# Modulation products moved between engines and stages, a new head for the first FFNs, and more PSUM banks in turn

## The chip, the cores and the metric

The kernel is one launch on one core of a Trainium2 chip. The metric is device time in microseconds, the median of several runs. The engines are TensorE (PE, matrix products; PEld is its loading of weights), VectorE (DVE), ScalarE (ACT), GpSimd (POOL) and SyncE (SP), whose queue issues the transfers. Each engine takes its instructions in order from its own queue and waits for others by semaphores. Matrix products write into PSUM, which the kernel splits into eight banks of 128x512 float32, and everything else lies in SBUF.

## The reference

A first block of two layers (a state space mixer beside latent attention, attention to a memory, a gated FFN), then a second block of two layers on the result (attention over neighbours or a window, a gated FFN), whose norms are modulated by a vector `c`, with a context stream `ctx` beside `x`. Everything is float32. Shapes: 512 tokens of 1024 for `x`, 256 for `ctx`, FFN width 2816, so `w_up` gives 2 x 22 tiles of 128 channels. The parts that the change touches:

```python
# first block, at the end of each layer
x = x + memory_attention(rmsnorm(x, g_q), rmsnorm(mem, g_kv), ...)
u = causal_dwconv(rmsnorm(x, norm_ffn[i]) @ w_up[i], conv_w, conv_b)   # 3 taps
gate, val = u[..., :D_FF], u[..., D_FF:]
x = x + (silu(gate) * val) @ w_down[i]
# second block, layer i: needs all six parts of mod, of x and (not in the last layer) of ctx
mod = silu(c) @ w_mod[i] + b_mod[i]            # 1024 -> 6 x 1024
mod_c = silu(c_ctx) @ w_mod[i] + b_mod[i]
sh1, sc1, gt1, sh2, sc2, gt2 = split(mod)
h = rmsnorm(x, g_attn[i]) * (1 + sc1) + sh1
x = x + gt1 * (attention(h, ...) @ w_out)
h = rmsnorm(x, g_ffn[i]) * (1 + sc2) + sh2
x = x + gt2 * conv_ffn(h, ...)                 # the same for ctx in layer 0
```

`mod` is a product of a matrix with one vector. The kernel computes it off TensorE: a tile of 128 rows and 512 columns of `w_mod` is multiplied by `silu(c)` element by element and summed along the row.

## The kernel before

Activations lie transposed, channels on partitions: `x` is eight tiles of 128 x 512 tokens. TensorE gets each float32 operand in two parts, a high half rounded to its format and a low half, the rest: for weights `wh` and `wl`, and likewise for activations (both named `A` in the traces, as most temporary tiles are). A product of one 128 x 128 weight block with one x tile is three matrix products: wh times high, wh times low, wl times high (`lin`, L298). A tile of 1024 inputs so takes 24 products. `wload` (L317) brings a weight tile into `wr` by an SP transfer, makes `wh` on ScalarE (L314) and `wl` on VectorE (L331); there are two `wr` and three each of `wh` and `wl`, so a tile's halves are made at most a few tiles ahead. `gsplit` (L437, L438) makes the halves of an x tile, scaled by the norm's gain.

In time order the program is: for each of two layers mixer, `mem_attn`, `ffn1`; then the context and neighbourhood attention of the second block, `attn_out`, `ffn2` for both streams, the window attention, `attn_out_halves`, `ffn2` for `x` alone.

`ffn1` (from L1155) runs `F1_PARTS`: 6, 6, 5 and 5 of the 22 gated pairs. A pair `j` is two up tiles (`up`): 24 products into a bank (`L`, `S`, `PT` in turn), on VectorE a product with the norm's factor `rs` out of the bank (L1178), the first tap of the convolution on ScalarE (L1181), two taps on VectorE (L1183), then silu (L1185), gate (L1186) and the split (L314, L317). The down tiles of a part are queued and run between the pairs of the next part; each ends with an addition into `x` on VectorE (L1199). The sum of squares for the norm comes from GpSimd and ScalarE; TensorE adds it over the channels by products with `ones`, VectorE takes the inverse root in ten small steps on 128 x 4 numbers (`rt`, L394, L369 to L379), and TensorE spreads that over the partitions (`O<-cm,rt`). At the start of `ffn1` the first up tile waits for the last x tile of `mem_attn`, and the norm's spread is placed in the midst of the second tile.

The modulation is a side job: `mod_steps` (L1250) is a generator, and `step(n, r)` takes from it at fixed places of other stages, with `after` holding the instruction back to the matrix product issued before it. Of eight products two are a `scalar_tensor_tensor` with a sum on VectorE (L1282), six a GpSimd product (L1284) with a copy and sum on ScalarE behind it (L1262). Layer 0 of the first block makes all of `mod[0]`, layer 1 all of `mod[1]`: one step for each of the eight `w_mo` tiles of `mem_attn`, then 2 or 5 a pair in `ffn1`. The tiles of `w_mod` are loaded four steps ahead, into the pool of 59 `A` tiles.

`ffn2` (L2000) in layer 0 has both streams: an up weight tile serves 24 products 256 wide (`ctx`) and 24 products 512 wide (`x`). Its parts are 8, 7 and 7 pairs, then 16 down outputs each. All go through two buffers of bank `L`. At the end of a part `lins` runs the first down outputs without the last activation tile, then that tile's products.

The order of each engine's instructions around these places is fixed by a scheduler at build time, from the order of the code and the holds.

Of the kernel before, what the change touches and what calls it, by code (L numbers as in the profile page):

```python
# [14 lines left out]
AF = mybir.ActivationFunctionType  # L15
# [21 lines left out]
PSTEP = (5,3,1)  # L37
MSTEP = (0,1,4,1,2)
MDN = (0,0,2)
MH = 48  # L40
MLAG = 3
FX = 1
# [19 lines left out]
PIN = 1  # L62
MPF = 4
MODV = (0,4)
WP = 0
# [21 lines left out]
F1_PARTS = ((0, 6), (6, 6), (12, 5), (17, 5))  # L87
F1_MOD = (2, 5, 5, 5)
F1_KEEP = 2
# [169 lines left out]
class Builder:  # L259
# [263 lines left out]
    def mixer(self, i, f, fn):  # L523
# [215 lines left out]
        for tb in range(4):  # L739
            row = []  # L740
            for hf in range(2):
                ps = self.p("S")
                for k in range(2):
                    ch, cl = ckh[k]
                    s = slice(tb * P, tb * P + P)
                    w = slice(k * 512, k * 512 + 512)
                    self.mm(ps, ch[:, s], wv[hf][0][:, w], k == 0, False)
                    self.mm(ps, ch[:, s], wv[hf][1][:, w], False, False)
                    self.mm(ps, cl[:, s], wv[hf][0][:, w], False, k == 1)
                vt = self.t("A", [P, S])  # L750
                nc.scalar.activation(vt, ps, AF.Copy)
                row.append(vt)
            V.append(row)
# [310 lines left out]
    def mem_attn(self, i, f, mh, K, fn):  # L1064
# [16 lines left out]

        self.steps = self.mod_steps(i, 0, 96)
        mv = self.mem_v(i, mh, V)
# [64 lines left out]


    def step(self, n, r):  # L1150
# [6 lines left out]
    def ffn1(self, i, f, fn):  # L1157
# [3 lines left out]
        self.wp = WP  # L1161
        self.bank = 0

        def bank():
            self.bank += 1
            return self.p(FTAGS[self.bank % len(FTAGS)])

        def up(j):
            ab = []
            for e in range(2):  # L1170
                ct = j + NFF * e
                ps = bank()
# [72 lines left out]

    def mod_steps(self, i, n0, n1):
        nc = self.nc
        cv = []
        for v in range(2):
            for e in range(2):  # L1250
# [4 lines left out]
            yield  # L1255
        part = self.mparts
        late = []

        def add(k):
            while len(late) > k:  # L1260
                o, t = late.pop(0)
                nc.scalar.activation(t, t, AF.Copy, accum_out=o)  # L1262

        ws = {}

        def load(n):
            if n < n1:
                ws[n] = self.t("A", [P, 512])
                nc.sync.dma_start(out=ws[n], in_=self.a["w_mod"][i, n // 2, n % 2])

        for n in range(n0, n0 + MPF):
            load(n)
        for n in range(n0, n1):
            load(n + MPF)
            m, e = divmod(n, 2)
            w = ws.pop(n)
            for v in range(2):
                t = self.t("A", [P, 512])
                self.modn += 1
                o = part[:, v, e, m:m + 1]  # L1280
                if self.modn % 8 in MODV:
                    nc.vector.scalar_tensor_tensor(out=t, in0=w, scalar=1.0, in1=cv[2 * v + e], op0=ALU.mult, op1=ALU.mult, accum_out=o)  # L1282
# [3 lines left out]
            add(MLAG)  # L1286
            yield
        add(0)
        if n1 == 96:
            for v in range(2):  # L1290
                mo = self.mod[i][:, :, v]
                nc.vector.tensor_add(out=mo, in0=part[:, v, 0], in1=part[:, v, 1])
                nc.vector.tensor_add(out=mo, in0=mo, in1=self.v(f"b_mod{i}"))
            for j, gn in ((0, "g_attn"), (1, "g_ffn")):
                for s in range(2):
                    nc.vector.scalar_tensor_tensor(out=self.G[i][j][:, :, s], in0=self.mod[i][:, 24 * j + 8:24 * j + 16, s], scalar=1.0,
                                                   in1=self.v(f"{gn}{i}"), op0=ALU.add, op1=ALU.mult)
            yield
# [640 lines left out]

    def out_it(self, i, m, ox, k0, k1):  # L1940
        n = k1 - k0
        w = self.wload(self.a[f"w_o2{i}"][m, :, k0 * P:k1 * P], n * P)
        ps = self.p("L")
        yield from self.lin_it(ps, w, ox[k0:k1])
        self.nc.vector.scalar_tensor_tensor(out=self.x[:, m], in0=ps, scalar=self.msl(i, 2, m, 0), in1=self.x[:, m], op0=ALU.mult, op1=ALU.add)
# [54 lines left out]
    def ffn2(self, i, rx, rc, acc, accc, steps=iter(()), late=None):  # L2000
# [3 lines left out]
        if rc is not None:  # L2004
            streams[1] = (rc, ML)
        w, ab = {}, {}

        def up(j, e, s, tag="L"):
# [3 lines left out]
            ps = self.p(tag)  # L2012
            self.lin(ps[:, :n], w[j, e], rhs)
# [21 lines left out]

        for pi, (j0, nj) in enumerate(FF_PARTS):
            act = {s: [] for s in streams}
            last = pi == len(FF_PARTS) - 1
            first = 0
            if pi == 0 and rc is not None and FX:  # L2040

                for j, e, s in ((0, 0, 1), (0, 1, 1), (1, 0, 1), (0, 0, 0), (0, 1, 0), (1, 1, 1), (1, 0, 0), (1, 1, 0)):
                    up(j, e, s, "S" if s else "L")
                    if e == 1:
# [31 lines left out]
            def down(m, s):  # L2076
# [3 lines left out]
                else:  # L2080
                    ps = self.p("L")
                    self.lin(ps[:, :n], weights(m), act[s])
# [10 lines left out]
            for z, (m, s) in enumerate(order[:DW]):  # L2093
                pss[m, s] = self.p(DT2[z % len(DT2)])
# [79 lines left out]
    def build(self):  # L2174
        self.setup()
        self.modn = 0
        self.mod_prep()
# [46 lines left out]
```

## Time and profile before

| | us |
|---|---|
| median of 3 runs | 3841.25 |
| lowest and highest | 3839.11, 3844.32 |
| profiled execution | 3832.78 |
| its span | 3831.0 |
| PE busy | 3675.2 (96%) |
| DVE busy | 2669.1 (70%) |
| ACT busy | 1842.9 (48%) |
| POOL busy | 1001.0 (26%) |

The profile is of one execution. Its span goes from the first to the last instruction; the profiled execution's time lies 1.8 us above it. A row of a stretch gives for each engine the busy time and, in brackets, the number of instructions; PEclk is the granted clock as a share of 2.4 GHz. In a timeline, brackets tell how long the engine stood idle before the instruction and what released it.

### The profile page before, as it was taken

The numbers are of one execution on the slowest core, as the hardware profiler recorded it, in microseconds if no ns is written. First come the engines' busy times: TensorE is split into PE (matmuls) and PEld (weight loads), VectorE is DVE, ScalarE is ACT, GpSimd is POOL, SyncE is SP. The second block draws the span as 40 slices with busy tenths as digits, with TensorE's granted clock in tenths as the row PEclk, the third lists the DMA queues.
The fourth block names the chain that finished last, engine by engine and source line by source line (L and its number), as shares of the span: only waits on it lengthen the run. The fifth ranks groups of instructions, "written<-read, shape, count | busy, mean of one in ns | idle before, by whom it ended". The sixth has DMA issues, their size and how long they took to land. (4 is left out here: it accounts for less than half of the span.)

```text
span 3831.0 us, 55553 instructions
## 1 busy us (share of the span) xinstructions
PE 3675.2 (96%) x21300; PEld 3062.5 (80%) x21300; DVE 2669.1 (70%) x4599; ACT 1842.9 (48%) x3532; POOL 1001.0 (26%) x688
## 2 busy tenths in 40 slices
PE   8999999999899999999999899899999999999999
PEld 6777788777778777887777899778888888888887
DVE  7768756889977687668998753777545547657555
ACT  5645634455555456344555454774222225554232
POOL 1223243467621121234666212321000012100000
PEclk9999999999999999999999999999999999999999
DMA  3222143344422211333444332322212212012232
GB/s 112 67 72 67 51 127 100 111 154 157 146 91 72 72 57 56 126 105 102 165 155 150 123 104 92 108 73 72 66 61 61 66 56 74 15 40 93 94 95 93
DMA packets 128714, 354.39 MB, mean 93 GB/s; under 512 B 14144, under 2 KB 26816, under 8 KB 128448
## 3 DMA queue, kind: packets, MB, share of 16 engines
q1 hardware_dynamic: 127440, 349.62, 28.6%
q8 instruction: 168, 2.75, 0.3%
q10 hardware_dynamic: 1008, 1.21, 0.1%
q14 instruction: 98, 0.80, 0.1%
HBM read 346.58 MB, written 4.19 MB: 92 GB/s over the span
## 5 line engine op out<-in xcount | busy, mean ns | idle before, releaser
L304 PE MATMUL L<-A,wh 128*128 128x512 f32 (+1 forms) x6408 | 1861.5, 375 | 19.5 <-ACT wh L314 8.8
L304 PEld LDWEIGHTS L<-A,wh 128*128 128x128 f32 x6408 | 1148.0, 189 | 241.7 <-ACT wh L314 13.1
L304 PE MATMUL L<-A,wl 128*128 128x512 f32 (+1 forms) x3204 | 1194.9, 373 | 20.4 <-DVE wl L331 19.8
L314 ACT ACTIVATE wh<-wr 128x1024 fp32r<-128x1024 f32 (+4 forms) x562 | 561.9, 1001 | 787.7 <-PE L L304 429.8
L331 DVE TENSOR_TENSOR wl<-wr,wh 128x1024 fp32r<-128x1024 f32 (+4 forms) x503 | 658.7, 1311 | 327.2 <-ACT wh L314 319.1
L304 PEld LDWEIGHTS L<-A,wl 128*128 128x128 f32 x3204 | 604.7, 189 | 137.5 <-DVE wl L331 26.3
L1284 POOL TENSOR_TENSOR A<-A,A 128x512 f32<-128x512 f32 x288 | 482.3, 1706 | 280.6 <-DMA A<-in_w_mod 169.2
L304 PE MATMUL S<-A,wh 128*128 128x512 f32 (+1 forms) x944 | 301.0, 400 | 25.6 <-ACT wh L314 14.7
L331 POOL TENSOR_TENSOR wl<-wr,wh 128x1024 fp32r<-128x1024 f32 (+1 forms) x59 | 139.4, 2363 | 547.4 <-ACT wh L314 473.4
L304 PE MATMUL L<-wh,A 128*128 128x256 f32 x1440 | 272.7, 285 | 2.3 <-ACT A L1309 2.0
L304 PE MATMUL PT<-A,wh 128*128 128x512 f32 (+1 forms) x904 | 262.1, 375 | 0.0
L304 PEld LDWEIGHTS S<-A,wh 128*128 128x128 f32 x944 | 180.9, 195 | 70.8 <-ACT wh L314 16.5
L1183 DVE SCALAR_TENSOR_TENSOR A<-A,vec,A 128x512 f32<-128x512 f32 x176 | 215.2, 1223 | 30.6 <-ACT A L1181 26.4
L304 PEld LDWEIGHTS L<-wh,A 128*128 128x128 f32 x1440 | 226.0, 189 | 8.1 <-issue 4.2
L304 PE MATMUL O<-A,A 128*64 128x128 f32 (+3 forms) x2528 | 228.1, 288 | 4.2 <-DVE A L648 3.6
L433 POOL TENSOR_TENSOR acc<-acc,A 128x512 f32<-128x512 f32 (+1 forms) x44 | 53.8, 1222 | 672.1 <-ACT A L427 670.2
L304 PE MATMUL L<-wl,A 128*128 128x256 f32 x720 | 204.6, 284 | 4.6 <-DVE wl L331 4.6
L304 PEld LDWEIGHTS O<-A,A 128*64 128x64 f32 (+1 forms) x2528 | 168.5, 143 | 48.6 <-issue 24.0
L304 PE MATMUL S<-A,wl 128*128 128x512 f32 (+1 forms) x472 | 189.8, 402 | 17.8 <-DVE wl L331 17.6
L1262 ACT ACTIVATE A<-A 128x512 f32<-128x512 f32 x288 | 177.3, 618 | 38.5 <-POOL A L1284 38.3
L304 PEld LDWEIGHTS PT<-A,wh 128*128 128x128 f32 x904 | 166.7, 191 | 32.7
L314 ACT ACTIVATE A<-A 128x512 fp32r<-128x512 f32 (+2 forms) x202 | 115.3, 571 | 147.4 <-DVE A L1186 78.1
(323 smaller groups left out, 5249.7 us busy)
## 6 DMA issues: line engine op xcount, KB each, us to landing
wr<-in_w_up SPq DMA_DIRECT2D x176, 512.0 KB
A<-in_w_mod SPq DMA_DIRECT2D x192, 256.0 KB
wr<-in_w_qkv SPq DMA_DIRECT2D x62, 512.0 KB
wr<-in_w_in SPq DMA_DIRECT2D x60, 512.0 KB
wr<-in_w_down SPq DMA_DIRECT2D x32, 448.0 KB
wr<-in_w_down SPq DMA_DIRECT2D x32, 384.0 KB
wr<-in_w_down SPq DMA_DIRECT2D x32, 320.0 KB
wr<-in_w_os SPq DMA_DIRECT2D x16, 512.0 KB
```

The costliest lines, as they stand in the source:

```text
L304: self.last_mm = self.nc.tensor.matmul(out, lhsT=l, rhs=r, start=start, stop=stop, skip_group_check=True)
L314: self.nc.scalar.activation(h, src, AF.Copy)
L331: eng.tensor_sub(out=l[:, :cols], in0=r[:, :cols], in1=h[:, :cols].bitcast(F32))
L433: self.mark_p = (add or nc.gpsimd).tensor_add(out=acc.t, in0=acc.t, in1=dst)
L1183: ve.scalar_tensor_tensor(out=ac, in0=u[:, tap:tap + S], scalar=cw(tap), in1=ac, op0=ALU.mult, op1=ALU.add)
L1262: nc.scalar.activation(t, t, AF.Copy, accum_out=o)
L1284: nc.gpsimd.tensor_mul(out=t, in0=w, in1=cv[2 * v + e])
```

## The change

It has these parts.

- Modulation: all products go to VectorE; the generator goes through one half of the inputs (`e`) and then the other, loads two steps ahead, and leaves out the two thirds of layer 1's `mod_c` that nothing uses. Each first block layer makes half of `mod[0]`; `mod[1]` is made in `ffn2` of layer 0. The rates are 0.5 a `w_mo` tile, 1 and 2.5 a pair in `ffn1`, 0.7 an up tile and 1.2 a down output in `ffn2`.
- `ffn1` starts with `up_head`: two tiles without the last x tile, then that tile's products for both, and the norm's spread in the third tile.
- `ffn2` of layer 0 has four parts like `ffn1` and takes `L`, `S`, `PT` in turn; the second half of `attn_out` does too. The value projection takes `S` and `PT` in turn.

```diff
-MSTEP = (0,1,4,1,2)
+MSTEP = (0,0.5)
-MPF = 4
-MODV = (0,4)
+MPF = 2
-F1_MOD = (2, 5, 5, 5)
+F1_MOD = (1, 2.5, 2.5, 2.5)
+F2_PARTS = ((0, 6), (6, 6), (12, 5), (17, 5))
+F2_MOD = (0.7, 1.2)
...
-                ps = self.p("S")
+                ps = self.p(("S", "PT")[hf])
...
-        self.steps = self.mod_steps(i, 0, 96)
+        self.steps = self.mod_steps(0, 24 * i, 24 * i + 24)
...
+        def up_head():
+            parts = [(bank(), self.wload(a[f"w_up{i}"][z // 2, z % 2]), f.rhs) for z in range(2)]
+            self.lins(parts)
+            st = self.rstd_a(f.acc, D)
+            ps = bank()
+            for k, _ in enumerate(self.lin_it(ps, self.wload(a[f"w_up{i}"][1, 0]), f.rhs)):
+                if k == 4:
+                    with self.after():
+                        rf.append(st())
+            return {(0, 0): parts[0][0], (0, 1): parts[1][0], (1, 0): ps}
...
-                self.lin(ps, self.wload(a[f"w_up{i}"][j, e]), f.rhs)
-                if not rf:
-                    rf.append(self.rstd_of(f.acc, D))
...
-                if self.modn % 8 in MODV:
-                    nc.vector.scalar_tensor_tensor(out=t, in0=w, ..., in1=cv[2 * v + e], ..., accum_out=o)
-                else:
-                    nc.gpsimd.tensor_mul(out=t, in0=w, in1=cv[2 * v + e])
-                    late.append((o, t))
+        nv = lambda m: 2 if i < DEPTH - 1 or m < 16 else 1
+        for e in range(2):
...
+            for m in range(m0, m1):
+                load(m + MPF)
+                w = ws.pop(m)
+                for v in range(nv(m)):
+                    t = self.t("A", [P, 512])
+                    nc.vector.scalar_tensor_tensor(out=t, in0=w, scalar=1.0, in1=cv[v], op0=ALU.mult, op1=ALU.mult,
+                                                   accum_out=part[:, v, e, m:m + 1])
+                yield
...
-            for _ in self.out_it(i, m, ox, 4, 8):
+            for _ in self.out_it(i, m, ox, 4, 8, self.next_bank):
...
+        bank = self.next_bank if both else lambda: self.p("L")
+        fparts = F2_PARTS if both else FF_PARTS
+        if both:
+            self.bank = 0
+            self.steps = self.mod_steps(1, 0, 48)
...
                     for s in sorted(streams, reverse=True):
                         up(j, e, s)
+                        if both and j < j0 + nj - 1:
+                            self.step(4 * j + 2 * e + 1 - s, F2_MOD[0])
...
                 down(m, s)
+                if both:
+                    self.step(n, F2_MOD[1] if pi < 3 else 100)
```

On PE, at the start of layer 0's `ffn1`, the first up tile goes into an `S` bank, the second into `PT`, the third into `L`; the last x tile's halves are `A_6220` and `A_6221`. Before:

```order
L304 MATMUL S_6256<-A_6221,wh_6258 128x512
L304 MATMUL S_6256<-A_6220,wl_6259 128x512
L304 MATMUL O_6287<-ones,acc_4938 128x1 x4
L304 MATMUL PT_6317<-A_5894,wh_6319 128x512
...
L304 MATMUL PT_6317<-A_6080,wh_6319 128x512
L304 MATMUL PT_6317<-A_6081,wh_6319 128x512
L304 MATMUL O_6303<-cm,rt_6292 128x128 x4
L304 MATMUL PT_6317<-A_6080,wl_6320 128x512
```

And now, where the last x tile's halves are `A_6193` and `A_6194` and the tile before it is `A_6154`:

```order
L304 MATMUL S_6228<-A_6154,wl_6231 128x512
L304 MATMUL PT_6235<-A_5894,wh_6237 128x512
...
L304 MATMUL PT_6235<-A_6154,wl_6238 128x512
L304 MATMUL S_6228<-A_6193,wh_6230 128x512
L304 MATMUL S_6228<-A_6193,wl_6231 128x512
L304 MATMUL PT_6235<-A_6193,wh_6237 128x512
L304 MATMUL PT_6235<-A_6193,wl_6238 128x512
L304 MATMUL O_6290<-ones,acc_4938 128x1 x4
L304 MATMUL L_6306<-A_5894,wh_6308 128x512
...
L304 MATMUL L_6306<-A_6109,wl_6309 128x512
L304 MATMUL O_6328<-cm,rt_6295 128x128 x4
```

The first two tiles run their first seven x tiles before either meets the last one; the norm's products with `ones` follow both, and its spread (`cm,rt`) stands behind 18 products of the third tile.

On VectorE, in the third part of layer 0's `ffn1`, one pair with its down tile. `mparts` marks a modulation product, 128x1024 an up weight, 128x640 a down weight. Before:

```order
L331 TENSOR_TENSOR wl_9224<-wr_9222,wh_9223 128x1024
L1183 SCALAR_TENSOR_TENSOR A_9114<-A_9111,vec,A_9114 128x512 x2
L1199 TENSOR_TENSOR x<-x,L_9160 128x512
L1186 TENSOR_TENSOR A_9114<-A_9076,A_9114 128x512
L331 TENSOR_TENSOR wl_9295<-wr_9293,wh_9294 128x640
L317 TENSOR_TENSOR A_9121<-A_9114,A_9120 128x512
L1282 SCALAR_TENSOR_TENSOR A_9136,mparts<-A_8997,A_5947 128x512
L1282 SCALAR_TENSOR_TENSOR A_9151,mparts<-A_9012,A_5947 128x512
L1177 MEMSET A_9214 128x2
L1178 TENSOR_TENSOR A_9214<-S_9183,rs_6308 128x512
```

And now, with line numbers 16 higher (L1194 is L1178 of before, L1199 is L1183, L1215 is L1199):

```order
L331 TENSOR_TENSOR wl_8692<-wr_8690,wh_8691 128x1024
L1199 SCALAR_TENSOR_TENSOR A_8600<-A_8597,vec,A_8600 128x512 x2
L1215 TENSOR_TENSOR x<-x,L_8628 128x512
L1202 TENSOR_TENSOR A_8600<-A_8562,A_8600 128x512
L331 TENSOR_TENSOR wl_8746<-wr_8744,wh_8745 128x640
L317 TENSOR_TENSOR A_8607<-A_8600,A_8606 128x512
L1289 SCALAR_TENSOR_TENSOR A_8612,mparts<-A_8493,A_7533 128x512
L1289 SCALAR_TENSOR_TENSOR A_8614,mparts<-A_8493,A_7536 128x512
L1289 SCALAR_TENSOR_TENSOR A_8618,mparts<-A_8499,A_7533 128x512
L1289 SCALAR_TENSOR_TENSOR A_8620,mparts<-A_8499,A_7536 128x512
L1289 SCALAR_TENSOR_TENSOR A_8624,mparts<-A_8610,A_7533 128x512
L1289 SCALAR_TENSOR_TENSOR A_8626,mparts<-A_8610,A_7536 128x512
```

Where two modulation products stood behind the split, six stand now; the other steps are the same.

On VectorE, in the down outputs behind the first part of layer 0's `ffn2`. Before:

```order
L331 TENSOR_TENSOR wl_26133<-wr_26131,wh_26132 128x1024
L2084 SCALAR_TENSOR_TENSOR A_18674<-L_26014,mod_108,A_18674 128x256
L2084 SCALAR_TENSOR_TENSOR x<-L_26046,mod_108,x 128x512
L331 TENSOR_TENSOR wl_26191<-wr_26189,wh_26190 128x1024
L2084 SCALAR_TENSOR_TENSOR A_18674<-L_26072,mod_108,A_18674 128x256
L2084 SCALAR_TENSOR_TENSOR x<-L_26104,mod_108,x 128x512
L331 TENSOR_TENSOR wl_26249<-wr_26247,wh_26248 128x1024
```

And now (L2097 is L2084 of before, an output added into `x` or, in `A`, into the context):

```order
L2097 SCALAR_TENSOR_TENSOR A_17802<-PT_24896,mod_108,A_17802 128x256
L1289 SCALAR_TENSOR_TENSOR A_24932,mparts<-A_24890,A_24138 128x512
L1289 SCALAR_TENSOR_TENSOR A_24956,mparts<-A_24922,A_24135 128x512
L1289 SCALAR_TENSOR_TENSOR A_24958,mparts<-A_24922,A_24138 128x512
L331 TENSOR_TENSOR wl_24963<-wr_24961,wh_24962 128x768
L1289 SCALAR_TENSOR_TENSOR A_24988,mparts<-A_24928,A_24135 128x512
L2097 SCALAR_TENSOR_TENSOR x<-L_24934,mod_108,x 128x512
L1289 SCALAR_TENSOR_TENSOR A_25012,mparts<-A_24954,A_24135 128x512
L331 TENSOR_TENSOR wl_25017<-wr_25015,wh_25016 128x768
```

Modulation products, each with its own transferred tile, now stand between the outputs and ahead of the low halves of the weights, and the banks rotate.

## Rows read from the trace of the kernel before

**Rows 1.** The page, busy time, share of the span, instructions per engine.

```profile
PE 3675.2 (96%) x21300; PEld 3062.5 (80%) x21300; DVE 2669.1 (70%) x4599; ACT 1842.9 (48%) x3532; POOL 1001.0 (26%) x688
```

**Rows 2.** Windows: length; PE, PEld, DVE, ACT, POOL busy (count); PEclk, DMA share, GB/s.

```profile
670.90:1083.40 412.50, 383.92 (x1608) 305.88 (x1608) 365.56 (x460) 220.58 (x450) 255.86 (x155) 0.97 0.44 140
1719.10:2140.40 421.30, 389.61 (x1614) 310.41 (x1613) 362.56 (x472) 224.83 (x466) 243.27 (x147) 0.96 0.43 138
2606.00:3160.00 554.00, 552.09 (x3130) 480.47 (x3131) 306.93 (x665) 161.16 (x264) 13.01 (x11) 1.00 0.20 62
3480.00:3800.00 320.00, 320.00 (x1379) 258.58 (x1378) 197.18 (x330) 107.28 (x145) 0.00 (x0) 1.00 0.31 96
```

**Rows 3.** Windows of 40 us in layer 0's first and second FFN.

```profile
900.00:940.00 40.00, 40.00 (x174) 32.37 (x173) 36.74 (x43) 22.07 (x46) 27.46 (x17) 1.00 0.53 169
1020.00:1060.00 40.00, 35.05 (x140) 27.56 (x139) 34.78 (x55) 21.50 (x48) 17.85 (x12) 0.91 0.36 105
2640.00:2680.00 40.00, 39.98 (x228) 34.64 (x227) 27.66 (x65) 14.27 (x26) 0.00 (x0) 1.00 0.22 66
```

**Rows 4.** PE's waits, 670 to 1090: total us, times, longest.

```profile
PE S L304 <- DVE wl L331: 8.1, 4, 3.6
PE L L304 <- DVE wl L331: 7.5, 5, 3.0
```

**Rows 5.** VectorE groups, 720 to 1080: busy us, mean ns | idle before, releasers.

```profile
L1183 DVE SCALAR_TENSOR_TENSOR A<-A,vec,A 128x512 f32<-128x512 f32 x80 | 100.0, 1249 | 13.1 <-ACT A L1181 11.5 <-issue 0.2
L331 DVE TENSOR_TENSOR wl<-wr,wh 128x1024 fp32r<-128x1024 f32 x37 | 57.9, 1564 | 9.4 <-ACT wh L314 9.4
L1282 DVE SCALAR_TENSOR_TENSOR A<-A,A 128x512 f32<-128x512 f32 x43 | 54.7, 1299 | 0.0
```

**Rows 6.** VectorE groups in layer 1's second FFN, 3480 to 3800.

```profile
L2027 DVE SCALAR_TENSOR_TENSOR A<-A,vec,A 128x512 f32<-128x512 f32 x84 | 63.1, 752 | 2.5
L331 DVE TENSOR_TENSOR wl<-wr,wh 128x1024 fp32r<-128x1024 f32 x48 | 58.7, 1225 | 47.2 <-ACT wh L314 46.3
```

**Rows 7.** VectorE's timeline at 2071: start, us, engine, line, operation.

```profile
2071.19 0.68 DVE L1282 SCALAR_TENSOR_TENSOR A<-A,A 128x512 f32<-128x512 f32 x1
2071.81 0.68 DVE L1282 SCALAR_TENSOR_TENSOR A<-A,A 128x512 f32<-128x512 f32 x1
```

**Rows 8.** Windows of both first FFNs' heads.

```profile
675.80:692.40 16.60, 8.53 (x27) 6.28 (x25) 12.86 (x24) 4.12 (x8) 13.37 (x10) 0.79 0.12 36
1725.50:1738.20 12.70, 8.28 (x24) 6.36 (x25) 11.33 (x16) 1.78 (x4) 10.56 (x8) 0.73 0.13 42
```

**Rows 9.** Timelines of ACT, DVE and PE in layer 0's head.

```profile
675.13 0.63 ACT L1262 ACTIVATE A<-A 128x512 f32<-128x512 f32 x1 [4.39 <-POOL A L1284]
685.47 1.32 DVE L369 TENSOR_SCALAR rt<-rt 128x4 int32<-128x4 int32 x1
692.13 0.16 DVE L379 SCALAR_TENSOR_TENSOR rt<-rt 128x4 f32<-128x4 f32 x1
692.44 1.13 PE L304 MATMUL O<-cm,rt 128*128 128x128 f32 x8 [3.33 <-DVE rt L379]
```

**Rows 10.** PE's waits in layer 0's value projection, 250 to 270.

```profile
PE S L304 <- ACT A L751: 2.1, 1, 2.1
```

**Rows 11.** PE's waits in layer 0's output projection, 2566 to 2608.

```profile
PE L L304 <- DVE x L1945: 3.7, 2, 2.8
```

**Rows 12.** PE and DVE timelines, end of the second FFN's first part.

```profile
2745.06 0.40 PE L304 MATMUL L<-A,wl 128*128 128x512 f32 x1
2751.91 0.69 DVE L317 TENSOR_TENSOR A<-A,A 128x512 fp32r<-128x512 f32 x1 [0.70 <-ACT A L314]
2752.96 0.63 PE L304 MATMUL L<-A,wh 128*128 128x512 f32 x2
```

**Rows 13.** The page's group of GpSimd products: busy, mean | idle, releaser.

```profile
L1284 POOL TENSOR_TENSOR A<-A,A 128x512 f32<-128x512 f32 x288 | 482.3, 1706 | 280.6 <-DMA A<-in_w_mod 169.2
```

**Rows 14.** PE's waits in layer 1's first FFN, 1719 to 2142.

```profile
PE O L304 <- DVE acc L433: 3.1, 1, 3.1
```

More of the change, by code (lines that the diff above doesn't have):

```diff
@@ L1147, in mem_attn, with next_bank @@
             self.step(m, MSTEP[1])
+    def next_bank(self):
+        self.bank += 1
+        return self.p(FTAGS[self.bank % len(FTAGS)])
     def step(self, n, r):
@@ L1162, in ffn1 @@
         self.bank = 0
-        def bank():
-            self.bank += 1
-            return self.p(FTAGS[self.bank % len(FTAGS)])
+        bank = self.next_bank
+        def up_head():
[8 more added lines that the diff above has]
+            return {(0, 0): parts[0][0], (0, 1): parts[1][0], (1, 0): ps}
+        early = up_head()
         def up(j):
@@ L1171, in up @@
                 ct = j + NFF * e
-                ps = bank()
-                self.lin(ps, self.wload(a[f"w_up{i}"][j, e]), f.rhs)
-                if not rf:
-                    rf.append(self.rstd_of(f.acc, D))
+                ps = early.pop((j, e), None)
+                if ps is None:
+                    ps = bank()
+                    self.lin(ps, self.wload(a[f"w_up{i}"][j, e]), f.rhs)
                 u = self.t("A", [P, S + 3])
@@ L1243, in mod_prep, with mod_steps @@
         self.G = [[self.c([P, KD, 2], name=f"G{i}{j}") for j in range(2)] for i in range(DEPTH)]
-    def mod_steps(self, i, n0, n1):
+    def mod_steps(self, i, m0, m1):
         nc = self.nc
-        cv = []
-        for v in range(2):
-            for e in range(2):
+        part = self.mparts
+        nv = lambda m: 2 if i < DEPTH - 1 or m < 16 else 1
+        for e in range(2):
+            cv = []
+            for v in range(2):
                 c = self.t("A", [P, 512])
@@ L1254, in mod_steps @@
                 cv.append(c)
[L1255 to L1272, printed above, removed]
@@ L1288, in mod_steps, with load @@
[L1288 to L1293, printed above, removed]
+            ws = {}
+            def load(m):
+                if m < m1:
+                    ws[m] = self.t("A", [P, 512])
+                    nc.sync.dma_start(out=ws[m], in_=self.a["w_mod"][i, m, e])
+            for m in range(m0, m0 + MPF):
+                load(m)
@@ new lines, in mod_steps @@
+            for m in range(m0, m1):
[6 more added lines that the diff above has]
+                yield
+        if m1 == 48:
+            for v in range(2):
+                n = 48 if nv(47) > v else 16
+                mo = self.mod[i][:, :n, v]
+                nc.vector.tensor_add(out=mo, in0=part[:, v, 0, :n], in1=part[:, v, 1, :n])
+                nc.vector.tensor_add(out=mo, in0=mo, in1=self.v(f"b_mod{i}")[:, :n])
@@ L1294, in mod_steps @@
             for j, gn in ((0, "g_attn"), (1, "g_ffn")):
-                for s in range(2):
-                    nc.vector.scalar_tensor_tensor(out=self.G[i][j][:, :, s], in0=self.mod[i][:, 24 * j + 8:24 * j + 16, s], scalar=1.0,
+                for v in range(2 if j == 0 else nv(47)):
+                    nc.vector.scalar_tensor_tensor(out=self.G[i][j][:, :, v], in0=self.mod[i][:, 24 * j + 8:24 * j + 16, v], scalar=1.0,
                                                    in1=self.v(f"{gn}{i}"), op0=ALU.add, op1=ALU.mult)
@@ L2006, in ffn2, with up @@
         w, ab = {}, {}
-        def up(j, e, s, tag="L"):
+        both = rc is not None
+        bank = self.next_bank if both else lambda: self.p("L")
[3 more added lines that the diff above has]
+            self.steps = self.mod_steps(1, 0, 48)
+        def up(j, e, s):
             rhs, n = streams[s]
@@ L2011, in up @@
                 w[j, e] = self.wload(a[f"w_up2{i}"][j, e])
-            ps = self.p(tag)
+            ps = bank()
             self.lin(ps[:, :n], w[j, e], rhs)
@@ L2034, in gate @@
             return self.split(A)
-        for pi, (j0, nj) in enumerate(FF_PARTS):
+        for pi, (j0, nj) in enumerate(fparts):
             act = {s: [] for s in streams}
-            last = pi == len(FF_PARTS) - 1
+            last = pi == len(fparts) - 1
             first = 0
@@ L2080, in down @@
                 else:
-                    ps = self.p("L")
+                    ps = bank()
                     self.lin(ps[:, :n], weights(m), act[s])
@@ L2093, in ffn2 @@
             for z, (m, s) in enumerate(order[:DW]):
-                pss[m, s] = self.p(DT2[z % len(DT2)])
+                pss[m, s] = bank()
             self.lins([(pss[m, s][:, :streams[s][1]], weights(m), act[s]) for m, s in order[:DW]])
```

18 lines of the change are left out of this document (3 added, 15 removed).

## The prediction

> **What bounds the kernel now.** The profile was read in this order: the page's busy times, then the stretches by stage, then PE's waits in the stages that lose time, then the VectorE groups in a stage that loses against one that does not, then the timeline at the places where PE stands.
>
> PE is busy for 96% of the span, so what can be won is the few per cent in which it stands or runs slowly, and the question is where these lie [rows 1]. A stretch without loss gives the measure: in the second FFN of layer 1, PE is busy for all of 320.00 us and passes 1379 products, 320.00 / 1379 = 0.232 us each [rows 2]. By this the first FFN of layer 0, 412.50 us with 1608 products, needs 1608 x 0.232 = 373.1 and loses 39.4 us; that of layer 1, 421.30 us with 1614, needs 374.5 and loses 46.8. Together 86 us (the few one-column products are counted as full ones; a few missing records would lower the loss by as little). The second FFN of layer 0 loses almost nothing: 552.09 of 554.00 us are busy [rows 2].
>
> Within a first FFN the loss is not even: 900 to 940 is whole (174 products), 1020 to 1060 has 140 and a granted clock of 0.91, that is, part of it at 1.2 GHz instead of 2.4 [rows 3]. In layer 0 PE waits 8.1 and 7.5 us for `wl` from VectorE, the low halves of weight tiles [rows 4]. VectorE is late there because it is long: beside GpSimd's work its convolution step takes 1249 ns, a 1024 wide `wl` 1564, a modulation product 1299 [rows 5]. The same two kinds take 752 and 1225 in layer 1's second FFN, where GpSimd does nothing [rows 6], and three modulation products in a row follow each other at 0.62 us where GpSimd is between two of its own [rows 7]. So GpSimd's products cost PE time through VectorE, though GpSimd is never waited for in the long term.
>
> At the start of each first FFN comes another loss: 16.60 us with 27 products and 12.70 with 24 [rows 8], that is 16.60 - 6.26 = 10.3 and 12.70 - 5.57 = 7.1, 17.4 of the 86. ScalarE stands 4.39 us for a GpSimd product ahead of the last x tile's high half, for which PE waits; the norm's four-column steps, 0.16 us where undisturbed, take up to 1.32; PE stands 3.33 us for the norm [rows 9].
>
> **The change part by part.** All sums are against the profiled execution, 3832.78 us; the median of the three runs, 3841.25, lies 8.5 above it, and the forecast adds that back.
>
> Modulation. 288 GpSimd products of 1706 ns [rows 13] and their 288 sums on ScalarE go; the 96 VectorE products become 320: 96 in each first FFN's stretch and 128 in the second FFN of layer 0. VectorE in the first FFN of layer 0 is busy 365.56 us now [rows 2]. Its products there go from some 48 at 1.30 (62 us) to some 96 at 0.62 (60), which adds nothing; some 88 convolution steps lose 0.50 each (44) and 37 `wl` 0.34 each (12.5), so about 308 us in a stage of some 376, 82% against 89%, and the other steps shorten too. Ahead of a late `wl` stand as a rule four convolution steps and another `wl`, 4 x 0.50 + 0.34 = 2.3 us less, and the waits are 8.1 / 4 and 7.5 / 5, 1.5 to 2 each [rows 4]. Of the body's loss (86.2 - 17.4 = 68.8 us, some 6 of it at the end of layer 1's, below) I let 4 of 62.8 remain: gain 59. Bounds: 0 remain, or half of it (31), since products stand in clumps of 4 to 6 in VectorE's queue, 2.5 to 3.7 us, with `wl` and the next convolution behind them, and PE behind these.
>
> The end of layer 1's first FFN. PE waits 3.1 us for the context's sum of squares [rows 14] and runs slowly after it, about 6 in all; that work stays, only its neighbours shorten. I take half, 3, between 0 and 6.
>
> Head. Two tiles run 42 products without the last x tile, 42 x 0.232 = 9.7 us of cover where there were 21 (4.9); the last x tile's high half no longer has a GpSimd product ahead of it. These waits should go. What is late next is the norm: its spread stands behind 18 products, 4.2 us. The chain of ten small steps of 0.16 us, each with a short pause behind it, is about 2.0 us undisturbed (an estimate), and two `wl` of 1.2 lie between its steps: 4.4 us; so PE may stand 0 to 1.5 us. I leave 3 of 17.4 for both layers: gain 14.5, bounds 9 to 17.
>
> V projection. PE waits 2.1 us for a copy out of bank S once in a layer [rows 10]; with PT in turn a copy has twice the time. Gain 4 to 6, with the slow stretch behind the wait; 5 taken; 0 if the copies themselves are too slow.
>
> Output projection of layer 0. PE waits 3.7 us in two places for VectorE to free L [rows 11]; three banks hide a late one. 3 taken, between 0 and 3.7.
>
> Second FFN of layer 0. 128 products of 0.62 are 79 us on VectorE in 554, and eight more output steps per stream. Beside up products VectorE is busy 27.66 of 40 us now [rows 3]; with 2.8 steps of one or two products in the 2 x 24 x 0.348 = 16.7 us of an up pair, 1.7 to 3.5 us, it comes to 32 to 36. In down stretches it has more room. The parts, 6, 6, 5, 5 instead of 8, 7, 7, have a price of their own: after the last up product of a part (2745.06) its activation's low half starts at 2751.91 and ends 0.69 later, 7.1 us after the product's end, and the next product that needs it starts at 2752.96 [rows 12], so the cover was some 0.4 us too long. With six tiles the first products of two outputs cover 5 x 3 x (0.116 + 0.232) + 0.35 = 5.6 us (0.116, half of 0.232, for a 256 wide one), with five 4.5; the order moves a few up products behind, 0.5 to 1.4. So waits of up to 1.3, 1.3, 2.5 and 1 appear. Cost 2 to 25, 5 taken.
>
> Sum: -59 - 3 - 14.5 - 5 - 3 + 5 = -79.5. 3832.8 - 79.5 = 3753.3 profiled, 3762 as median.
>
> **Two rules weighed.** That a VectorE product on two SBUF tensors may pass at full rate is shown by the spacing of 0.62 us for 512 elements [rows 7]. The Trainium skill, "Vector Engine (DVE) Microarchitecture Reference", section "Points that are easy to get wrong", says the opposite: a scalar_tensor_tensor whose two SBUF sources are not bf16 runs at half throughput. By that rule each product would take twice 0.62, 198 us more over 320 of them, the body of the first FFNs would gain nothing, and the sum would be -20.5 instead of -79.5. The trace does not bear it out.
>
> Rotating three PSUM banks leaves PE whole from 900 to 940, where up and down tiles go through L, S and PT in turn: 40.00 us busy, 174 products, clock 1.00 [rows 3]. The Trainium skill, "TensorE: Matmul & The Clock Gate", section "A second HAM failure mode: psum-queue depth-cycling", warns that cycling through banks makes PE idle in small gaps and its clock swing. By the rule the new rotation would lower the clock of the second FFN; by the row it costs nothing, and the sum takes nothing.
>
> **Rivals.** One: VectorE becomes the bound. One engine in order now carries conversions, convolutions and products; clumps stand ahead of `wl`. For it: losses come where VectorE is 87% busy (34.78 of 40 from 1020 [rows 3]). Against it: from 900 to 940 it is busy 36.74 and PE loses nothing. Half the body's loss stays (27 more than forecast) and the second FFN loses 20 instead of 5: -79.5 + 27 + 15 = -37.5, median 3804.
>
> Two: GpSimd is not the cause of the long steps, or the products take 1.24 us each on VectorE. For it: other things differ in these stages too, the DMA engines are busy for 0.44 of the time there and 0.30 in the clean stretch [rows 2]. Against it: the spacing of 0.62 in the midst of such a stage [rows 7]. Then VectorE stays as full as now, and the gain is heads 14.5, V 5, output 3, end 3, minus 5: -20.5, median 3821.
>
> Three, slower: VectorE waits for modulation weights. GpSimd stood 169.2 us for them over the whole run [rows 13]; there it blocked nobody but ScalarE, now a late transfer holds every `wl` behind it, and only two are ahead instead of four. Against it: a product's place is now spaced over up tiles, some 6 us apart, and the queue may load early. VectorE has (376 - 308) / 48 = 1.4 us of slack for each transfer in a first FFN; the gain of 79.5 over 192 transfers is 0.4 each; so from about 1.8 us of lateness on every transfer it turns. At 2.3 us: 192 x 0.5 = 96 lost beyond the gain, about 3937; at 1.9, 3860.
>
> **How the numbers follow.** Forecast 0.65 (its own range 3745 to 3785), rival one 0.18, rival two 0.07, rival three 0.06, and 0.04 for sums of small costs that end near the old time. A difference under 0.2% (7.7 us) can't be told from none here. Faster holds the forecast, rivals one and two, less 0.02 of their far ends: 0.88; within 0.2%: 0.05; slower: 0.07. The range goes from all upper gains, 3832.8 - (69 + 17 + 6 + 3.7) + 2 + 8.5 = 3748 less 6 for records miscounted, 3742, to just past rival one, 3808; beyond lie rivals two and three and a little below.
>
> **What would show it.** Right: in both first FFNs convolution steps near 0.75 us and 1024 wide `wl` near 1.23, the stages near 375 and 385 us, PE's waits for `wl` nearly gone, clock at 1.00; at the head one short wait for the norm. In the second FFN of layer 0 waits under 3 us at four ends of parts, and the stage at 556 to 562. Wrong: convolution steps still over 1.1 us without GpSimd beside them (rival two); VectorE above 90% and PE waiting for `wl` (one); VectorE waiting for a transfer from `w_mod` ahead of a `wl` (three).

## The result

The changed kernel takes 3753.01 us (median of 4 runs, 3746.41 to 3762.11) against 3840.18 (4 runs) before: ratio 0.9774, 95% interval 0.975 to 0.9798. The forecast was 3762, in a range from 3742 to 3808. The profiled execution, 3762.11, is the slowest of the four, with a span of 3760.3; the one before, 3832.78, lies below all four runs of its kernel. So the spans of the two profiles lie 70.7 us apart, and the medians 87.2.

The page after, and the windows of the two first FFNs and of layer 0's second FFN, cut at the same instructions as in [rows 2] (length; PE, PEld, DVE, ACT, POOL busy; PEclk, DMA share, GB/s):

```profile
PE 3656.6 (97%) x21300; PEld 3059.4 (81%) x21300; DVE 2618.3 (70%) x5070; ACT 1673.9 (45%) x2968; POOL 524.6 (14%) x400
```

```profile
671.10:1043.70 372.60, 372.60 (x1619) 302.36 (x1618) 292.00 (x539) 138.44 (x176) 23.59 (x16) 1.00 0.40 125
1687.50:2060.00 372.50, 371.54 (x1622) 301.21 (x1621) 290.30 (x558) 143.68 (x192) 11.81 (x8) 1.00 0.39 126
2530.90:3087.60 556.70, 556.20 (x3146) 485.96 (x3147) 391.53 (x951) 163.21 (x274) 12.90 (x11) 0.99 0.34 109
```

The first FFN of layer 0 fell from 412.50 to 372.60 us, and PE is busy in all of it; that of layer 1 fell from 421.30 to 372.50. Together these are 88.7 us, of 86 thought to be lost. The span fell by 70.7; where the other 18 us went is told below.

VectorE's groups in layer 0's first FFN, 720 to 1040, against [rows 5] (line, tile, count | busy, mean ns | idle before):

```profile
L1199 DVE SCALAR_TENSOR_TENSOR A<-A,vec,A 128x512 f32<-128x512 f32 x76 | 56.7, 750 | 3.6 <-ACT A L1197 2.1
L1289 DVE SCALAR_TENSOR_TENSOR A<-A,A 128x512 f32<-128x512 f32 x83 | 52.8, 688 | 0.1
L331 DVE TENSOR_TENSOR wl<-wr,wh 128x1024 fp32r<-128x1024 f32 x35 | 43.3, 1238 | 6.8 <-ACT wh L314 6.7
```

Convolution steps went from 1249 ns to 750 and 1024 wide `wl` from 1564 to 1238, near the durations of [rows 6]; products went from 1299 to 688. PE's waits from 640 to 1050, against [rows 4], are two in all:

```profile
PE L L304 <- DVE A L438: 0.8, 1, 0.8
PE O L304 <- POOL acc L433: 0.4, 1, 0.4
```

### The profile page after: what moved, and what is told of

Read it like the earlier page. It is cut to its first block, busy times and chain, and to the rows that moved or that the text cites. A ratio compares the mean times of both kernels' runs of the same rounds, so it can differ in the third digit from the quotient of the medians.

```text
span 3760.3 us, 54839 instructions
## 1 busy us (share of the span) xinstructions
PE 3656.6 (97%) x21300; PEld 3059.4 (81%) x21300; DVE 2618.3 (70%) x5070; ACT 1673.9 (45%) x2968; POOL 524.6 (14%) x400
## 5 line engine op out<-in xcount | busy, mean ns | idle before, releaser
L304 PE MATMUL L<-A,wh 128*128 128x512 f32 (+1 forms) x5020 | 1509.0, 383 | 11.8 <-ACT wh L314 5.1
L304 PEld LDWEIGHTS L<-A,wh 128*128 128x128 f32 x5020 | 907.8, 189 | 196.2 <-issue 12.8
L304 PE MATMUL L<-A,wl 128*128 128x512 f32 (+1 forms) x2510 | 953.3, 380 | 5.6 <-DVE wl L331 4.9
L304 PEld LDWEIGHTS L<-A,wl 128*128 128x128 f32 x2510 | 473.9, 189 | 102.2 <-DVE wl L331 7.5
L304 PE MATMUL S<-A,wh 128*128 128x512 f32 (+1 forms) x1608 | 469.5, 375 | 11.6 <-ACT wh L314 9.1
L304 PE MATMUL PT<-A,wh 128*128 128x512 f32 (+1 forms) x1628 | 439.3, 357 | 1.0 <-DVE x L1949 0.9
L304 PE MATMUL PT<-A,wl 128*128 128x512 f32 (+1 forms) x814 | 290.3, 357 | 1.0 <-DVE wl L331 1.0
L1289 DVE SCALAR_TENSOR_TENSOR A<-A,A 128x512 f32<-128x512 f32 x320 | 213.0, 706 | 7.2 <-DMA A<-in_w_mod 5.5
L2038 DVE SCALAR_TENSOR_TENSOR A<-A,vec,A 128x512 f32<-128x512 f32 (+1 forms) x264 | 173.6, 661 | 5.0
L304 PEld LDWEIGHTS S<-A,wl 128*128 128x128 f32 x804 | 152.8, 190 | 28.7 <-DVE wl L331 0.8
```

Source lines behind the costliest of these rows:

```text
L304: self.last_mm = self.nc.tensor.matmul(out, lhsT=l, rhs=r, start=start, stop=stop, skip_group_check=True)
L2038: ve.scalar_tensor_tensor(out=ac, in0=u[:, tap:tap + n], scalar=cw(tap), in1=ac, op0=ALU.mult, op1=ALU.add)
```

## The experiments

All times are medians in us, and ratios are to the kernel before, which took 3835 to 3840 beside them. The theory after the result is that GpSimd's modulation products lengthened VectorE's steps, and VectorE made PE late. The rivals are that fewer products in a stage did it, or that ScalarE was freed of their sums, or the new head.

**Idle products on GpSimd.** Added to the changed kernel:

```diff
+                if i == 0:
+                    for v in (0, 1, 0):
+                        nc.gpsimd.tensor_mul(out=self.t("A", [P, 512]), in0=w, in1=cv[v])
```

> The changed kernel with three GpSimd products beside every modulation step of the first FFNs (144 a layer, as many as before the change), whose results nothing reads. Theory (GpSimd's products lengthen VectorE's two-input steps, and that was the loss): the convolution step goes from 0.75 to about 1.25 us again, PE waits for wl come back, each first FFN loses some 20 to 30 us, in all 3753 + 40 to 60 = 3793 to 3813. Rival (the gain came from fewer modulation products in a stage and from ScalarE's sums leaving): nobody waits for these products, so 3753 within 8.

Measured 3901.51 (3898.58 to 3907.36), slower than before the change: ratio 1.0165, 1.0148 to 1.0182. Its groups of VectorE and GpSimd from 720 to 1040, then the window of layer 0's first FFN, 439 us long:

```profile
L1289 DVE SCALAR_TENSOR_TENSOR A<-A,A 128x512 f32<-128x512 f32 x74 | 88.1, 1235 | 1.8 <-ACT A L1273 1.8
L1199 DVE SCALAR_TENSOR_TENSOR A<-A,vec,A 128x512 f32<-128x512 f32 x70 | 80.7, 1160 | 4.6 <-ACT A L1197 3.5
L1293 POOL TENSOR_TENSOR A<-A,A 128x512 f32<-128x512 f32 x111 | 193.9, 1778 | 132.9 <-DMA A<-in_w_mod 74.7 <-DVE A L1289 21.0 <-PE PT L304 11.1
```

```profile
671.00:1110.00 439.00, 390.50 (x1610) 307.56 (x1609) 406.40 (x539) 136.49 (x176) 261.96 (x155) 0.96 0.34 106
```

Nothing reads these products, and the same steps are long again. VectorE's timeline beside nine of them, and then GpSimd's:

```profile
926.41 1.77 DVE L1289 SCALAR_TENSOR_TENSOR A<-A,A 128x512 f32<-128x512 f32 x1
928.12 0.68 DVE L1215 TENSOR_TENSOR x<-x,S 128x512 f32<-128x512 f32 x1
```

```profile
922.73 15.65 POOL L1293 TENSOR_TENSOR A<-A,A 128x512 f32<-128x512 f32 x9 [11.53 <-DMA A<-in_w_mod]
```

The modulation product has both inputs in SBUF and takes 1.77 us; the output step L1215, with one of its two inputs in the PSUM bank `S`, stays at 0.68 in the midst of the same GpSimd products. The cost, some 148 us over the changed kernel, was 2.5 to 3.7 times the 40 to 60 that I wrote; a part of that is that VectorE's own products, more than before, are lengthened too (1235 ns).

**The control on ScalarE.** The same three, as `nc.scalar.activation(self.t("A", [P, 512]), w, AF.Copy)`.

> The changed kernel with three ScalarE copies beside every modulation step of the first FFNs (144 a layer), whose results nothing reads: the control for the run with idle GpSimd products, with the same tiles, places and holds and another engine. Theory (GpSimd's products lengthen VectorE's steps): convolution steps stay at 0.75, ScalarE has the room (0.6 us each, 87 us in a stage of 375), so 3753 to 3765. Rival (any work on the modulation tiles at these places, by holding tiles or its engine's queue, delays the weights): near the 3901 of the idle GpSimd products.

Measured 3752.41 (3748.21 to 3758.07), convolution steps at 749 ns. Places, tiles and holds cost nothing that the time shows, so it is the engine.

**One input instead of two.** The same three, as `nc.gpsimd.tensor_copy(out=self.t("A", [P, 512]), in_=w)`.

> The changed kernel with three GpSimd copies (one input) instead of three GpSimd products (two inputs) beside every modulation step of the first FFNs. Theory (the two engines share a path for reads, and VectorE's two-input steps pay by the time GpSimd is busy): convolution steps still lengthened, by the copies' shorter time, 3800 to 3880. Rival (only a second input of GpSimd's collides): convolution steps at 0.75 and 3753 within 10.

Measured 3751.61 (3750.63 to 3758.29). The time is the rival's; the steps are the theory's, in small: convolution steps take 833 ns in the mean. VectorE's timeline beside three copies, then the copies, then the window of layer 0's first FFN:

```profile
915.68 0.69 DVE L1289 SCALAR_TENSOR_TENSOR A<-A,A 128x512 f32<-128x512 f32 x1
916.29 1.09 DVE L1289 SCALAR_TENSOR_TENSOR A<-A,A 128x512 f32<-128x512 f32 x1
917.32 1.08 DVE L1289 SCALAR_TENSOR_TENSOR A<-A,A 128x512 f32<-128x512 f32 x1
918.33 1.09 DVE L1289 SCALAR_TENSOR_TENSOR A<-A,A 128x512 f32<-128x512 f32 x1
919.35 0.68 DVE L1289 SCALAR_TENSOR_TENSOR A<-A,A 128x512 f32<-128x512 f32 x1
```

```profile
915.86 3.02 POOL L1293 COPY A<-A 128x512 f32<-128x512 f32 x3 [12.81 <-DVE A L317]
```

```profile
668.87:1041.26 372.39, 372.39 (x1616) 301.74 (x1615) 327.19 (x539) 139.19 (x176) 153.10 (x152) 1.00 0.40 126
```

A product takes 0.68 us alone, 1.09 beside a copy, and took 1.77 beside a GpSimd product. VectorE's work rose from 292 to 327 us, and PE, busy in all of 372.39, lost nothing: it pays only if VectorE's slack runs out.

**The old engines at the new rate.** Six of eight products of the first FFNs on GpSimd with their sums on ScalarE, the rest as changed:

```diff
+                    if i > 0 or self.modn % 8 in (0, 4):
+                        nc.vector.scalar_tensor_tensor(...)
+                    else:
+                        nc.gpsimd.tensor_mul(out=t, in0=w, in1=cv[v])
+                        late.append((o, t))
...
```

> The changed kernel with the old split of engines in the first FFNs alone: of eight products two on VectorE, six on GpSimd with the sum on ScalarE; rates, places and count (96 a layer) as changed. Theory (contention): 72 GpSimd products a layer instead of 144, so about half of the body's loss, 15 a layer, comes back: about 3753 + 30 = 3783 (3770 to 3800). Rival (the halved amount in a stage is what counts, not the engine): VectorE gets 45 us a layer freer, and the time is 3753 or a little less.

Measured 3753.07 (3751.8 to 3755.23): the rival's number. Its window of layer 0's first FFN, then its convolution steps:

```profile
671.00:1041.60 370.60, 370.18 (x1608) 300.38 (x1607) 285.37 (x406) 179.31 (x310) 125.91 (x82) 1.00 0.40 126
```

```profile
L1199 DVE SCALAR_TENSOR_TENSOR A<-A,vec,A 128x512 f32<-128x512 f32 x76 | 63.5, 835 | 7.3 <-ACT A L1197 5.8
```

Half of GpSimd's products still lengthen the steps (835 ns in the mean), yet they cost PE nothing: VectorE's work is 285 us where PE needs 370. My linear share, half the products for half the loss, was wrong.

**All on VectorE in the old places.** The kernel before with one line:

```diff
-MODV = (0,4)
+MODV = (0,1,2,3,4,5,6,7)
```

> The kernel before with one edit: all modulation products of the first FFNs on VectorE, at the old rates, places and count (192 a layer). Theory (contention costs, and VectorE's load has a limit): convolution steps at 0.75, but 192 x 0.62 = 119 us of products a layer fill VectorE to over 95% in the later parts, so PE waits for wl from there; 3790 to 3830, between the two kernels. Rival (VectorE's load alone was the bound before): slower than 3840, since VectorE gets 144 more products a layer than before.

Measured 3759.47 (3755.41 to 3761.64), ratio 0.9792 (0.9777 to 0.9806). Its window of layer 0's first FFN, its products from 720 to 1040, and PE's only wait for `wl` in it:

```profile
671.00:1046.50 375.50, 372.89 (x1614) 301.03 (x1613) 346.11 (x735) 138.10 (x174) 25.31 (x17) 1.00 0.47 154
```

```profile
L1282 DVE SCALAR_TENSOR_TENSOR A<-A,A 128x512 f32<-128x512 f32 x168 | 104.5, 685 | 0.0
```

```profile
PE S L304 <- DVE wl L331: 1.5, 1, 1.5
```

So one line gives 79 us, most of the gain, and more than my 3790 to 3830 allowed: VectorE is 92% busy, and PE stands under 3 us.

**Half on VectorE.** The kernel before with `MODV = (0,2,4,6)`.

> The kernel before with one edit: of eight modulation products four on VectorE and four on GpSimd, instead of two and six; old rates, places and count. Theory now (what counts is VectorE's own work, lengthened by GpSimd, against the 373 us that PE needs in a first FFN: 366 with six on GpSimd lost 40, 346 with none lost 3): here about 355, so a loss of 8 to 20 a layer, 3770 to 3800. Rival (the loss goes with GpSimd's products, 96 of 144 a layer): two thirds of some 80 stay, 3810.

Measured 3825.99 (3817.64 to 3832.42), ratio 0.9962 (0.9948 to 0.9976). Its window and its products:

```profile
671.00:1075.00 404.00, 378.92 (x1604) 301.35 (x1603) 365.12 (x550) 192.14 (x360) 176.94 (x107) 0.99 0.43 142
```

```profile
L1282 DVE SCALAR_TENSOR_TENSOR A<-A,A 128x512 f32<-128x512 f32 x84 | 99.2, 1228 | 0.0
```

The time lies above both forecasts. I had put VectorE's work at 355 us; it is 365, since a moved product is itself lengthened by those that stay (1228 ns). With that the stages line up roughly: VectorE's work in layer 0's first FFN of 285, 292, 327, 346, 365, 366 and 406 us goes with stages of 371, 373, 372, 376, 404, 412 and 439. Up to 346 the stage is PE's 370 to 376; at 365 it is some 30 longer. The sum is not all that counts: the kernel before does the same work, 365.56 us, in a stage 8 longer, and in layer 1, from norm to norm, this run has more work than the kernel before and the shorter stretch. The rows of layer 1, before and here:

```profile
1738.22:2120.30 382.08, 357.54 (x1486) 285.34 (x1487) 334.91 (x428) 208.80 (x438) 219.56 (x130) 0.96 0.44 145
1732.40:2109.32 376.92, 352.68 (x1485) 280.97 (x1486) 342.09 (x518) 181.37 (x348) 150.13 (x87) 0.98 0.44 146
```

No run fills VectorE to 365 us without GpSimd's products, so whether the sum or the clumps of long steps set the break is not shown.

**The old head.** The changed kernel with `early = {}` in place of `up_head()`, and the norm in the second tile again.

> The changed kernel with the first FFNs' old start: tile after tile with all eight x tiles, the norm's spread in the second. Prediction's term: the new head is worth 14.5 for both layers, so 3767. Rival (the old head lost only because ScalarE stood behind a GpSimd product and the norm's steps were long beside GpSimd): with GpSimd quiet the old head loses 1 to 3 a layer, so 3755 to 3759.

Measured 3752.27 (3748.46 to 3753.3), below the rival's range. The head's norm on PE, to be held against the 3.33 us in [rows 9]:

```profile
677.44 0.95 PE L304 MATMUL O<-ones,acc 128*128 128x1 f32 x8
682.16 1.13 PE L304 MATMUL O<-cm,rt 128*128 128x128 f32 x8 [0.19 <-DVE rt L379]
```

With GpSimd quiet, PE waits 0.2 us for the norm with the old head in this layer, and the new head adds nothing that the time shows.

**Old parts, one bank, in the second FFN.** Beside it the changed kernel again, 3754.61 (3752.75 to 3756.37):

```diff
-        bank = self.next_bank if both else lambda: self.p("L")
-        fparts = F2_PARTS if both else FF_PARTS
+        bank = lambda: self.p("L")
+        fparts = FF_PARTS
```

> The changed kernel as it is, in the same job as the two that follow, to compare with them: 3753 within 6, and its executions some 10 us apart.

> The changed kernel with the second FFN of layer 0 in its old three parts (8, 7, 7) and all outputs through bank L alone; the modulation of layer 1 stays in it. Prediction's terms: the four parts cost 3 to 6 us, so 3748 without them, unless two L buffers make VectorE's outputs late behind modulation products, which would cost 5 to 15: 3758 to 3768. Rival, from the profile of the changed kernel (PE stood 0.2 us in this whole stage): neither parts nor banks are worth anything, 3753 within 4.

Measured 3756.85 (3755.49 to 3758.05), ratio 0.9794 (0.9781 to 0.9808) beside 0.9787 (0.9774 to 0.9801): unclear by time. Its trace has one long wait in the stage, at its start. There the kernel before did not go through L alone, as its description above has it: the context tiles of its first two pairs went through S.

```profile
PE L L304 <- ACT A L2033: 8.8, 1, 8.8
```

From norm to norm the stage takes 565.36 us, and 555.42 in the unedited run beside it; the rest of this execution, where the two are alike, was as much shorter, so that the spans are level (3755.0 and 3754.6). The other waits for banks in the stage come to 1.5 us. So the two L banks are too few at the start, and behind it neither the parts nor the banks matter much; the start with S beside L was not tried.

**Two edits where the banks did not help.** The changed kernel with

```diff
-                nc.scalar.activation(vt, ps, AF.Copy)
+                nc.vector.tensor_copy(out=vt, in_=ps)
...
-            self.sumsq(acc, self.x[:, m], m == 0, m == KD - 1)
+            self.sumsq(acc, self.x[:, m], m == 0, m == KD - 1, add=self.nc.vector if m > 2 else None)
```

> The changed kernel with two edits where its trace shows what the banks did not cure: the value projection's copies out of PSUM on VectorE instead of ScalarE (ScalarE stood 2.00 us for another step ahead of them while PE waited 2.1), and the last sums of squares of layer 0's output projection added on VectorE instead of GpSimd (PE waited 4.30 for them). Theory: the waits go, with the slow clock behind them: 2 x (2 to 4) + 3 to 5, so 3753 - 7 to 13 = 3740 to 3746. Rival: PE waits there for what stands behind these steps anyway, 3753 within 4.

Measured 3744.69 (3743.21 to 3746.13), ratio 0.9763 (0.9749 to 0.9776), the fastest version. PE's waits for both in the whole run:

```profile
PE S L304 <- DVE A L751: 5.1, 2, 2.6
PE O L304 <- POOL acc L433: 0.4, 1, 0.4
```

The long wait for the sum (4.3) is gone; the copies' wait is longer than in the changed kernel (4.2), so the first edit gained nothing. From norm to norm the output projection took 29.35 us in the changed kernel's second profile and 23.03 here: 6.3 us are the sums'. The other 3 to 4 of the medians lie in stretches where the kernels are alike, so that the time met its forecast with one of the two terms at nothing.

**The two causes alone.** The kernel before with all products on VectorE and the last sums on VectorE.

> The kernel before with two edits alone: all modulation products on VectorE in their old places, and the last sums of squares of layer 0's output projection on VectorE. Theory (these are the two causes; head, rates, the move to the second FFN, banks and parts are worth next to nothing): the run with the first edit alone had 3759, the sums gave about 6 in the changed kernel, so 3750 to 3757, level with the whole change. Rival (in the kernel before, the two L buffers hold this stage, so the sums are not last): 3759 within 4.

Measured 3755.87 (3751.48 to 3760.68), ratio 0.9777 (0.9753 to 0.98): level with the whole change, and within both forecasts. In this kernel PE waits 3.8 us there for L, as in [rows 11], and the output projection takes 23.94 us from norm to norm, 23.91 in the kernel before: the sums give nothing here, as the rival has it. So the products' engine alone does nearly as much as the whole change.

## Why the prediction held, and which terms did not

*The body of the first FFNs* (59 forecast). The cause was as stated: durations fell to those of the clean stretch, and the idle products brought them back. But the size went by a poor measure. It set VectorE's work against the stage's own length (82% against 89%) and let some 10 us of the loss remain by guess, 4 in the body, 3 at the end of layer 1's and 3 in the heads; nothing remained. Set against the 373 us that PE needs, VectorE's work was 366 before, with hardly any slack, and came to 292 (308 forecast), with 81 us of it. That leaves rival one (VectorE becomes the bound) no room.

Rival two is refuted by the convolution steps at 750 ns and the products at 688. The trace before had told it too. The prediction reads three products at 0.62 us there; these are two, and the one ahead of them stood beside a GpSimd product, as VectorE's and GpSimd's timelines before show:

```profile
2069.48 1.78 DVE L1282 SCALAR_TENSOR_TENSOR A<-A,A 128x512 f32<-128x512 f32 x1
```

```profile
2065.66 5.06 POOL L1284 TENSOR_TENSOR A<-A,A 128x512 f32<-128x512 f32 x3 [1.41 <-DMA A<-in_w_mod]
2071.96 6.26 POOL L1284 TENSOR_TENSOR A<-A,A 128x512 f32<-128x512 f32 x4 [1.25 <-DVE A L1282]
```

The half throughput that the Trainium skill states for such steps ("Vector Engine (DVE) Microarchitecture Reference", "Points that are easy to get wrong") does not show here: a product takes 688 ns, no more than the gate's product of two tiles (L1202 after, 690 ns).

*Head* (14.5). The waits went, but not by the new order, as the run with the old head, no slower, shows: that term belongs to the first cause. The changed head's norm on PE, which does not wait for it; VectorE's ten steps and two `wl` lie between these two rows, as I had counted:

```profile
684.04 0.95 PE L304 MATMUL O<-ones,acc 128*128 128x1 f32 x8
689.26 0.91 PE L304 MATMUL O<-cm,rt 128*128 128x128 f32 x6
```

*V projection* (5). Nothing: PE waits 4.2 us in two places as before. ScalarE's and PE's timelines after:

```profile
257.38 0.63 ACT L427 ACTIVATE sq<-A 128x512 f32<-128x512 f32 x1 [2.00 <-DVE A L697]
258.53 0.57 ACT L751 ACTIVATE A<-S 128x512 f32<-128x512 f32 x1
259.16 0.50 PE L304 MATMUL S<-wh,A 128*128 128x512 f32 x1 [2.13 <-ACT A L751]
```

The row in [rows 10] named the copy, and I took the copy for slow, so that a second bank would give it time. It takes 0.6 us and was late: ScalarE stood 2.00 us for another step in front of it. On VectorE the copy stands behind a like step, so neither a further bank nor another engine cured it.

*Output projection* (3). Here a gain was forecast, and in this pair of profiles the change cost 5.4 us. PE's wait for a bank fell from 3.7 to 0.9, but the sum behind it became last. GpSimd's and PE's timelines after, PE's row for the same product before, and the windows from norm to norm, before and after:

```profile
2521.67 9.35 POOL L433 TENSOR_TENSOR acc<-acc,A 128x512 f32<-128x512 f32 x5 [3.87 <-ACT A L427]
2531.07 1.86 PE L304 MATMUL O<-ones,acc 128*128 128x1 f32 x8 [4.30 <-POOL acc L433]
2606.18 1.05 PE L304 MATMUL O<-ones,acc 128*128 128x1 f32 x8 [0.81 <-POOL acc L433]
```

```profile
2588.08:2611.99 23.91, 20.29 (x112) 17.00 (x112) 19.25 (x37) 11.51 (x20) 9.74 (x6) 1.00 0.37 121
2512.61:2541.95 29.34, 25.04 (x119) 22.14 (x119) 17.78 (x37) 11.38 (x20) 10.56 (x6) 0.83 0.30 97
```

Five dependent additions of 1.87 us follow the same late start as before, some 9 us behind the norm, so that PE gets the sum 18.5 us behind it, 18.1 before. PE came sooner, stood 4.30 us in one piece instead of 2.8 and 0.8, and then ran in part at half clock, 1.2 GHz (0.83 in the mean): from the sum to the next norm it took 10.9 us, 5.8 before. The stretch takes 26.6 to 29.6 us in all eight profiles with these banks and GpSimd's sums, and 23.9 to 25.2 in all four with L alone; with the new banks and the sums on VectorE it took 23.03. The rotation was not tried here by itself. The prediction failed to ask what is late next.

*Second FFN of layer 0* (cost 5). From norm to norm it took 555.97 us before and 555.46 after: no cost. The window of the result is 2.7 us longer because it takes in the slow clock ahead of the norm, just told. PE stood 0.2 us inside it; VectorE's work is 391.53 of 556.70, and no part's end shows the waits of up to 2.5 us that I had worked out, so the cover was longer than I counted.

The Trainium skill warns, from one kernel, that cycling through banks makes the clock swing ("TensorE: Matmul & The Clock Gate", "A second HAM failure mode: psum-queue depth-cycling"). The trace does not bear it out: the clock shows 1.00 in both first FFNs, where three banks turn, and 0.99 in this window.

*Rival three* (VectorE waits for modulation weights) showed once, in layer 0's second FFN, and PE did not stand for it; the other such wait in the run is 1.35 us, at 2664.86. VectorE's timeline after:

```profile
2588.75 0.69 DVE L1289 SCALAR_TENSOR_TENSOR A<-A,A 128x512 f32<-128x512 f32 x1 [4.16 <-DMA A<-in_w_mod]
```

So the cause was right, and that the total came so near is in part luck. It is a sum of wrong shares: about 12 too little from the first FFNs (88.7 against 76.5), 13 too much from the two bank terms (a gain of 8 forecast, a cost of some 5 measured), 5 too much of a cost for the second FFN. By the medians the gain is 87.2 us, 8 more than the 79.5 forecast.

Of the 18 us between the first FFNs' 88.7 and the span's 70.7, 5.4 are the output projection's. Some 8 lie in the mixer of layer 1 outside the value projection, where nothing was changed and PE's clock fell in this execution (0.94 and 0.97 in two windows of 60 us, 1.00 before). Two stretches there took 199.82 and 59.15 us from norm to norm, and 194.59 and 57.57 in the changed kernel's second profile, with the clock at 1.00: so 6.8 of the 8 are scatter. And 5.5 lie in the stretch from 2099.66 up to the norm in the output projection (412.95 us, 407.46 before), where PE waits some 3 us longer for `wl`. With the same code there, the eight other profiles took 407.6 to 412.3 us, and the four with the old code 407.3 to 410.3, so it is not shown that these 5.5 belong to the change.

## What to carry to other kernels

Sum the feeding engine's busy time per stage and set it against what the bound engine needs, not against the stage as it ran. Lengthening the feeder's steps cost nothing here as long as it had slack (up to 327 of 372 us with GpSimd beside it) and some 30 us at 365. Before a wait is cured with another buffer, look at what the awaited engine itself stood for, and at what is last once the buffer is there: in the output projection two short waits became one long one, and the time rose. A gain worked out for one edit may belong to another: the undone head and the one-line version show it. And before a stretch of one kernel is compared with that of another, look how far it lies apart in two profiles of the same one.

## What the runs showed of the hardware

A VectorE step with two SBUF inputs of 128x512 float32 takes 0.68 to 0.75 us alone, 1.09 beside a GpSimd copy and 1.77 beside a GpSimd product; GpSimd's product took 1.78 in the mean there, its copy 0.99. A step with one input in PSUM stayed at 0.68 beside GpSimd's products. ScalarE copies left the convolution step at 0.75.

Executions of one kernel lay up to 16 us apart (3746.41 to 3762.11), with granted clocks of 0.994 and 0.991. A wait of PE is followed by a stretch at half clock, 1.2 GHz, in one execution and not in another: behind the same 2.1 us in layer 0's value projection the clock was 0.83 from 256 to 266 in the changed kernel, and 1.00 from 253 to 263 with the idle ScalarE copies.
